# A bias table copied head by head within DRAM, and the last rows' final weighting taken apart, in a hybrid attention and mLSTM block

## The chip, the cores and the metric

The kernel runs on one core of a Trainium2 chip. The metric is the time of one execution on the device in microseconds (us). Engines are named as in the profile: PE (TensorE, matmuls), PEld (its weight loads), DVE (VectorE), ACT (ScalarE), POOL (GpSimd) and SP (SyncE, which here only issues DMAs).

## The reference, cut to what matters

One layer, 1024 rows of 1024 channels. The names that matter for the change are the relative-position bias, which is added to the scores of every head, and the last RMSNorm.

```
xn = rmsnorm(h, norm_w)
q, k, v, z, ml_q .. ml_z, ml_i, ml_f, gate_a, gate_m = split(xn @ w_in)
# differential attention, 8 heads, two score maps each
bias   = rel_bias[_rel_bucket(kpos - qpos)]            # 32 buckets x 8 heads
logits = q @ k.T + bias;  masked by chunks of 64
attn   = softmax(logits[0]) - lam * softmax(logits[1])
y_a    = rmsnorm(attn @ v, subln_w) * silu(z)
y_m    = mlstm(...) * silu(ml_z)
merged = sigmoid(gate_a) * (y_a @ w_pa) + sigmoid(gate_m) * (y_m @ w_pm)
h      = h + merged @ w_out
out    = rmsnorm(h, norm_final)
```

The bias depends on the distance between key and query alone, and is constant from a distance of 128 on. So one row of 384 numbers for each head holds it.

## The kernel before

Each projection is cut into *units* of 256 output columns: a unit's weights are loaded as two halves (`wt`, 3 buffers, L226), a power of two is found from their sum of squares (ACT L245 for the squares, DVE L159 for the sum `s`, one matmul with ones at L165, L135 to L139 for the scales `sb` and `isb`), and each half is split into a high and a low f16 part (`wp`, ACT L257 and DVE L259). Three matmuls replace one of f32 (`mm3`, L330 to L332; for units whose output stands in rows, L359 to L361). The units run in the order attention (for head h: `aqk` queries and keys, `avz` values and gate), attention gates, mLSTM, and so on; beside the units of head h+1 the attention of head h is computed, placed by a written list (PLAN_A). A scheduler then gives each engine a fixed order of instructions; engines wait for each other by semaphores. All DMAs of this part go out from SP, in SP's order: an issue that must wait holds those behind it.

`tables` (L408) makes the bias. A matmul gives `tb`, 8 heads on 8 partitions by 384 numbers (L428, L430, L431). One DMA (L433) writes it to DRAM as `tb_d`: each head's row of 1536 B 128 times, at a stride of 513 numbers. Read back at a stride of 512 (L590) this gives each of 128 query rows its own shift: the `strip` of a head, 128 x 256, two buffers. POOL scales it and puts the mask in (L591, L594), and the attention of that head begins with copying it into `BB` (DVE L806), from where L828 adds it to the scores. The projection of the input and forget gates (`if_proj`, L451; `wifp` is its weights' split) stands between the first two units.

The last stage (L1149 to L1179) multiplies by `w_out` in four blocks of 256 columns (`ch`), each over 8 row tiles (`tt`): L1170 adds the matmul's result to x in `xr`, L1171 sums its squares into `sso`. In the last block `factor` (L1131) makes the reciprocal root (a reduction on DVE, two small operations on POOL), and `finish` (L1138) weights the tile before: the left half on DVE, the right half on ACT and POOL, or on DVE too for the last tile; each half has its DMA (L1147).

Of the kernel before, what the change touches and what calls it, by code (L numbers as in the profile page):

```python
# [10 lines left out]
F32 = mybir.dt.float32  # L11
BF = mybir.dt.bfloat16
I32 = mybir.dt.int32
AF = mybir.ActivationFunctionType
ALU = mybir.AluOpType
AX = mybir.AxisListType

P = 128
S = 1024
D = 1024  # L20
NT = S // P
KC = D // P
H = 8
HD = 64
NB = 32
EPS = 1e-6
# [22 lines left out]
def block_kernel(ctx, tc, x, norm_w, w_in, lam, subln_w, rel_bias, conv_w, conv_b, b_if,  # L49
                 mh_w, b_gate, w_pa, w_pm, w_out, norm_final, onehot, out):  # L50
    nc = tc.nc
    v, s, g, te = nc.vector, nc.scalar, nc.gpsimd, nc.tensor
# [7 lines left out]
    dram = ctx.enter_context(tc.tile_pool(name="dram", bufs=1, space=bass.MemoryType.DRAM))  # L60
# [7 lines left out]
    def nm(p):  # L68
        uid[0] += 1
        return f"{p}{uid[0]}"  # L70

    def ctile(shape, dt=F32, p="c"):
        n = nm(p)
        return const.tile(shape, dt, tag=n, name=n)

    def R(dt=F32, shape=None, p="r"):
        return ring.tile(shape or [P, S], dt, tag="t4", name=nm(p))
# [7 lines left out]
    def sm(cols=1, dt=F32, p="s", bufs=6):  # L85
        return small.tile([P, cols], dt, tag=f"{p}{cols}", name=nm(p), bufs=bufs)

    def p_ps():
        return pp.tile([P, 512], F32, tag="pp", name=nm("pp"))
# [4 lines left out]
    def m_ps():  # L94
        return pmi.tile([P, 512], F32, tag="pmi", name=nm("pmi"))
# [4 lines left out]
    def junk(w):  # L100
        return wpool.tile([P, S], BF, tag="junk", name=nm("junk"), bufs=1)[:, :w]
# [171 lines left out]
    def wplain(w, i, c):  # L273
        hi, lo = w.parts[i // 2]
        return hi[:, i % 2, c], lo[:, i % 2, c]
# [127 lines left out]

    nlam = ctile([P, 1], p="nlam")
    lnc = ctile([P, 1], p="lnc")
    tb_d = dram.tile([H, P * 513], F32, tag="tbd", name="tb_d")

    def tables():  # L408
        oh = R(shape=[NB, 384], p="oh")
        nc.sync.dma_start(oh, onehot)  # L410
        lj = R(shape=[P, HD], p="lj")
        ls = sm(cols=2, p="ls")
        v.tensor_tensor_reduce(lj, lamb[:, 0, :], lamb[:, 1, :], 1.0, 0.0, op0=ALU.mult, op1=ALU.add,
                               accum_out=ls[:, 0:1])
        v.tensor_tensor_reduce(lj, lamb[:, 2, :], lamb[:, 3, :], 1.0, 0.0, op0=ALU.mult, op1=ALU.add,
                               accum_out=ls[:, 1:2])
        le = sm(cols=2, p="ls")
        s.activation(le, ls, AF.Exp)
        v.tensor_tensor(nlam, le[:, 1:2], le[:, 0:1], op=ALU.subtract)
        v.tensor_scalar(nlam, nlam, LAMBDA_INIT, None, op0=ALU.subtract)  # L420

        v.scalar_tensor_tensor(lnc, nlam, -1.0, nlam, op0=ALU.mult, op1=ALU.max)
        v.tensor_scalar(lnc, lnc, 1.0, 2.0 ** -5, op0=ALU.max, op1=ALU.mult)
        s.activation(lnc, lnc, AF.Ln)
        v.tensor_scalar(lnc, lnc, -1.0, None, op0=ALU.mult)
        yield
        tb_ps = m_ps()
        te.matmul(tb_ps[:H, :384], rb, oh, start=True, stop=True)  # L428
        tb = R(shape=[H, 384], p="tb")
        v.tensor_copy(tb, tb_ps[:H, :384])  # L430
        v.tensor_scalar(tb, tb, tb[:, 0:1], None, op0=ALU.subtract)  # L431

        nc.sync.dma_start(tb_d.rearrange("h (q u) -> h q u", u=513)[:, :, :384],  # L433
                    tb.unsqueeze(1).to_broadcast([H, P, 384]))
        yield
        cols_ps = m_ps()
        te.transpose(cols_ps[:, :NR], rows, ident[:NR, :NR])
        v.tensor_copy(cols, cols_ps[:, :NR])
        v.tensor_scalar(hb, cols[:, 88:104], 0.5, None, op0=ALU.mult)
        yield  # L440
# [116 lines left out]
    def sig_of(w):  # L557
        sg = sm(p="sig", bufs=8)
        v.tensor_tensor(sg, w.isb, isx, op=ALU.mult)
        return sg  # L560
# [18 lines left out]
    def c_aqk(h, w):  # L579
        sg = sig_of(w)  # L580
        v.tensor_scalar(sg, sg, 2.0 ** -60, None, op0=ALU.max)
        negc = sm(p="negc")
        v.scalar_tensor_tensor(negc, sg, -(2.0 ** 23), sg, op0=ALU.mult, op1=ALU.mult)
        sq = sm(p="sigm")
        v.tensor_tensor(sq, w.sb, sx, op=ALU.mult)
        v.tensor_scalar(sq, sq, 2.0 ** 60, None, op0=ALU.min)
        invc = sm(p="invc")
        v.scalar_tensor_tensor(invc, sq, 2.0 ** -23, sq, op0=ALU.mult, op1=ALU.mult)
        strip = ring.tile([P, 256], F32, tag="strip", name=nm("strip"), bufs=2)
        nc.sync.dma_start(strip, tb_d[h, :P * 512].rearrange("(q u) -> q u", u=512)[:, 127:383])  # L590
        g.tensor_scalar(strip, strip, invc, 1.0, op0=ALU.mult, op1=ALU.mult)  # L591
        mc = sm(p="mc")
        v.tensor_scalar(mc, invc, 2.0 ** 20, None, op0=ALU.min)
        g.tensor_scalar(strip[0:64, 192:256], maskv, mc[0:64, :], 1.0, op0=ALU.mult, op1=ALU.mult)  # L594
        Q = R(F16, [P, 2, S], p="Q")
        K = [R(F16, [P, 2, S], p="K") for _ in range(2)]
        live["qk", h] = (Q, K, negc, strip)
        hl = [None, None]
        done = [0, 0]

        def post(cb, th, ap):
            if hl[cb] is None:
                hl[cb] = R(F16, [P, 2, S], p="hl")
            t, x2 = HS[th], hl[cb]
            s.activation(x2[:, 0, t], ap, AF.Copy, scale=2.0 ** -13)
            v.scalar_tensor_tensor(x2[:, 1, t], ap, 2.0 ** -13, x2[:, 0, t], op0=ALU.mult,
                                   op1=ALU.subtract)
            done[cb] += 1
            if done[cb] == 2:
                for p in range(2):  # L610
                    src = x2[p * 64:p * 64 + 64]
                    for j in range(2):
                        if cb == 0:
                            nc.sync.dma_start(Q[j * 64:j * 64 + 64, p, :], src[:, j, :])
                        else:
                            nc.sync.dma_start(K[p][j * 64:j * 64 + 64, :, :], src)
        return None, post
# [162 lines left out]
    xr = []  # L780
# [278 lines left out]
    for _ in range(4):  # L1059
        first.prep_step()  # L1060
    weave(startup(0), first.prepping, normed(1))
    weave(startup(1), tables())


# [60 lines left out]
    nfb = BB  # L1125
    nc.sync.dma_start(nfb, norm_final.unsqueeze(0).to_broadcast([P, D]))
    sso = ctile([P, NT, 4], p="sso")
    last_bg.pop(0)()
    wo[0].finish_prep()

    def factor(tt):  # L1131
        rs = sm(p="xrs")
        v.tensor_reduce(rs, sso[:, tt, :], op=ALU.add, axis=AX.X)
        g.tensor_scalar(rs, rs, 1.0 / D, EPS, op0=ALU.mult, op1=ALU.add)
        g.tensor_tensor(rs, rs, mhalf[:, 0:1], op=ALU.pow)
        return rs

    def finish(tt, rs):  # L1138
        xt = xr[tt]
        for k in range(2):  # L1140
            c = HS[k]
            if k == 1 and tt < NT - 1:
                s.activation(xt[:, c], xt[:, c], AF.Copy, scale=rs)
                g.tensor_tensor(xt[:, c], xt[:, c], nfb[:, c], op=ALU.mult)
            else:
                v.scalar_tensor_tensor(xt[:, c], xt[:, c], rs, nfb[:, c], op0=ALU.mult, op1=ALU.mult)
            nc.sync.dma_start(out[0, tt * P:(tt + 1) * P, c], xt[:, c])  # L1147

    late = []  # L1149
    for ch in range(4):  # L1150
        w, so = wo[ch].w, [None, None]
        c = slice(ch * 256, ch * 256 + 256)
        n = 0
        for tt in range(NT):
            th, to = tt // 4, slice(tt % 4 * P, tt % 4 * P + P)
            ms = M[th][1]
            ps = p_ps()[:, :256]
            for _ in mm3(ps, KC, lambda i: (ms[i // 2][:, 0, i % 2, to], ms[i // 2][:, 1, i % 2, to]),
                         lambda i: wplain(w, i, slice(0, 256)), True, True):
                if last_bg:  # L1160
                    last_bg.pop(0)()
                n += 1
                if ch < 3 and n >= 2 and n % 3 == 0:
                    wo[ch + 1].start_prep()
                    wo[ch + 1].prep_step()
            if so[th] is None:
                so[th] = sm(p="so")
                v.tensor_tensor(so[th], w.isb, M[th][0], op=ALU.mult)
            xt = xr[tt]
            v.scalar_tensor_tensor(xt[:, c], ps, so[th], xt[:, c], op0=ALU.mult, op1=ALU.add)  # L1170
            s.activation(junk(256), xt[:, c], AF.Square, accum_out=sso[:, tt, ch:ch + 1])  # L1171
            if ch == 3:
                if len(late) > 0:
                    finish(*late.pop(0))
                late.append((tt, factor(tt)))
        if ch < 3:
            wo[ch + 1].finish_prep()
    for a in late:
        finish(*a)  # L1179

# [47 lines left out]
```

## Time and profile before

| | us |
|---|---|
| median of 3 runs (1415.33 to 1417.44) | 1416.35 |
| the profiled execution | 1417.01 |
| its span, first to last instruction | 1415.2 |
| PE busy | 1372.3 (97% of the span) |
| DVE busy | 848.1 (60%) |
| ACT busy | 734.3 (52%) |
| POOL busy | 157.1 (11%) |
| mean granted clock of PE | 0.993 of full speed |

The profile records one execution: for each engine when an instruction began and how long it took. An idle time is shown with the instruction that ended it. DMA share is the part of the time in which the core's 16 DMA engines were busy, on average. A busy PE is not the same as a fed PE, so the spacing of matmuls is read as well.

### The profile page before, as it was taken

To read this page: it belongs to the slowest core of one execution; us is meant where nothing else is said; L and a number is where in the kernel's file an instruction comes from. 1 tells how busy PE (TensorE), PEld (TensorE's weight loads), DVE (VectorE), ACT (ScalarE), POOL (GpSimd) and SP (SyncE) were. 2 spreads that over 40 slices of the span, in tenths; PEclk is the share of its full clock that TensorE was granted. 3 is DMA by queue.
4 is the path that set the end of the run, shared out by engine and by line. 5 is a ranking of instruction groups with operands and counts; after the bars stand their busy time and mean duration, and the time that the engine had idled before them with its cause. 6 is when DMAs were issued, how large, how long until landed. Compare 5 with 4: busy or idle time off the path is not lost.

```text
span 1415.2 us, 25057 instructions
## 1 busy us (share of the span) xinstructions
PE 1372.3 (97%) x9650; PEld 912.0 (64%) x9650; DVE 848.1 (60%) x2312; ACT 734.3 (52%) x1532; POOL 157.1 (11%) x215
## 2 busy tenths in 40 slices
PE   6979999999999999999999999999999999999997
PEld 3647576675765754444587696777768674444786
DVE  6267869769687677423627674765765654133633
ACT  7266657567675677622344443444435344544543
POOL 2001010010010001100102011020220200122004
PEclk9989999999999999999999999999999999999999
DMA  6557456474573534544221422322322135435203
GB/s 202 68 132 152 91 113 136 98 142 90 113 155 81 128 99 140 157 161 134 64 67 60 105 54 82 63 73 53 91 67 76 60 105 164 149 112 171 105 16 119
DMA packets 232761, 150.34 MB, mean 106 GB/s; under 512 B 117313, under 2 KB 209746, under 8 KB 232642
## 3 DMA queue, kind: packets, MB, share of 16 engines
q1 hardware_dynamic: 218482, 123.22, 35.5%
q10 hardware_dynamic: 14160, 25.53, 5.4%
q8 instruction: 75, 1.23, 0.4%
q14 instruction: 44, 0.36, 0.1%
HBM read 90.19 MB, written 18.68 MB: 77 GB/s over the span
## 4 chain that ended last, share of the span: by engine, by line
PE 78%; DVE 8%; DMA 5%; ACT 5%; issue 2%; POOL 2%; SPq 0%; POOLq 0%; DVEq 0%; ACTq 0%
PE pp L330 14%; PE pp L332 14%; PE pp L331 14%; PE pp L359 8%; PE pp L360 8%; PE pp L361 8%; PE psb L818 4%; DMA z<-z 2%; DMA wt<-in_w_in_dram 2%; DVE z L828 2%; ACT z L832 1%; DMA qw<-rows_d 1%; DVE z L851 1%; PE psb L914 1%; DVE wp L259 1%
## 5 line engine op out<-in xcount | busy, mean ns | idle before, releaser
L359 PE MATMUL pp<-wp,X 128*128 128x256 f16 x1280 | 350.2, 274 | 2.3 <-DVE tz L570 2.3
L361 PE MATMUL pp<-wp,X 128*128 128x256 f16 x1280 | 350.2, 274 | 0.0
L360 PE MATMUL pp<-wp,X 128*128 128x256 f16 x1280 | 350.2, 274 | 0.0
L332 PE MATMUL pp<-X,wp 128*128 128x512 f16 x768 | 291.0, 379 | 1.0 <-DVE wp L259 1.0
L330 PE MATMUL pp<-X,wp 128*128 128x512 f16 x768 | 291.5, 380 | 0.3 <-ACT wp L257 0.3
L331 PE MATMUL pp<-X,wp 128*128 128x512 f16 x768 | 291.5, 380 | 0.0
L257 ACT ACTIVATE wp<-wt,sb 128x512 f16<-128x512 f32 x208 | 137.5, 712 | 111.0 <-DVE sb L138 69.0
L245 ACT ACTIVATE junk<-wt 128x1024 bf16<-128x1024 f32 x112 | 118.2, 1056 | 115.6 <-DMA wt<-in_w_in_dram 105.2
L332 PEld LDWEIGHTS <-wp 128*128 128x128 f16 x1024 | 100.1, 98 | 119.1 <-DVE wp L259 1.5
L330 PEld LDWEIGHTS <-wp 128*128 128x128 f16 x1024 | 100.2, 98 | 101.8 <-issue 1.7
L331 PEld LDWEIGHTS <-wp 128*128 128x128 f16 x1024 | 100.1, 98 | 97.1
L259 DVE SCALAR_TENSOR_TENSOR wp<-wt,sb,wp 128x512 f16<-128x512 f32 x208 | 149.8, 760 | 13.4 <-ACT wp L257 11.8
L359 PEld LDWEIGHTS <-X 128*128 128x128 f16 x1280 | 125.7, 98 | 18.8 <-DVE tz L570 2.5
L360 PEld LDWEIGHTS <-X 128*128 128x128 f16 x1280 | 125.7, 98 | 16.0
L361 PEld LDWEIGHTS <-X 128*128 128x128 f16 x1280 | 125.7, 98 | 15.8
L832 ACT ACTIVATE z<-z,mx 128x256 f32<-128x256 f32 (+7 forms) x128 | 98.7, 772 | 46.9 <-DVE mx L831 27.4
L828 DVE CUSTOM_DVE_ANT_0 z<-psb,BB,negc 128x256 f32<-128x256 f32 (+7 forms) x128 | 104.1, 814 | 13.8 <-PE psb L818 13.7
L332 PE MATMUL pp<-Y,wp 128*128 128x512 f16 x256 | 97.0, 379 | 0.0
L331 PE MATMUL pp<-Y,wp 128*128 128x512 f16 x256 | 97.0, 379 | 0.0
L330 PE MATMUL pp<-Y,wp 128*128 128x512 f16 x256 | 97.0, 379 | 0.0
L655 DVE SCALAR_TENSOR_TENSOR acc<-up,wcol,acc 128x512 f32<-128x512 f32 x96 | 78.1, 828 | 27.1 <-POOL acc L656 24.8
L818 PE MATMUL psb<-K,Q 128*128 128x512 f16 (+3 forms) x384 | 83.3, 325 | 8.1 <-DVE mx L828 3.8
(253 smaller groups left out, 2005.0 us busy)
## 6 DMA issues: line engine op xcount, KB each, us to landing
wt<-in_w_in_dram SPq DMA_DIRECT2D x128, 256.0 KB, 3.3
wt<-in_w_in_dram SPq DMA_DIRECT2D x24, 512.0 KB
K<-hl SPq DMA_DIRECT2D x32, 256.0 KB, 4.2
gate_d<-tg ACTq DMA_DIRECT2D x32, 256.0 KB, 2.4
xt<-in_x_dram SPq DMA_DIRECT2D x8, 512.0 KB, 5.3
Q<-hl SPq DMA_DIRECT2D x32, 128.0 KB, 2.6
wt<-in_w_pa_dram SPq DMA_DIRECT2D x8, 512.0 KB, 3.8
ft<-gate_d ACTq DMA_DIRECT2D x16, 256.0 KB, 2.7
```

Of the source, the lines that this page charges most:

```text
L245: s.activation(j, w.wt[k], AF.Square, accum_out=ss[:, k:k + 1])
L257: s.activation(dst[0], src, AF.Copy, scale=w.sb)
L259: v.scalar_tensor_tensor(dst[1], src, w.sb, dst[0], op0=ALU.mult, op1=ALU.subtract)
L330: te.matmul(ps, wh, xh, start=(start and i == 0), stop=False, **kw)
L331: te.matmul(ps, wh, xl, start=False, stop=False, **kw)
L332: te.matmul(ps, wl, xh, start=False, stop=(stop and i == n - 1), **kw)
L359: te.matmul(ps[:, o], xh[:, t], wh, start=i == 0, stop=False)
L360: te.matmul(ps[:, o], xh[:, t], wl, start=False, stop=False)
L361: te.matmul(ps[:, o], xl[:, t], wh, start=False, stop=i == KC - 1)
L818: te.matmul(sp[:, c:e], Q[:, p, i * P:(i + 1) * P], K[p][:, j, c:e], start=(j == 0), stop=(j == 1))
L828: v.tensor_tensor_reduce(z[:, :n], sp[:, :n], bb[:, S - n:], negc, BIG, op0=ALU.add, op1=ALU.min, accum_out=mx)
L832: s.activation(z[:, :n], z[:, :n], AF.Exp, bias=mx, scale=-1.0, accum_out=rr[:, 2 * i + p:2 * i + p + 1])
```

## The change

**The table.** `tb` (8 rows of 384) goes to DRAM once, as `tbs_d`. A new function `table(h)` copies row h from there 128 times into a DRAM tensor of its own, `tb_d[h]`, with the stride of 513 as before. `table(0)` is called in `tables`, `table(h + 1)` behind the strip load of head h.

**The last rows.** For the last row tile the sum over the first three blocks, its scale and the product of columns 0 to 767 with `norm_final` are made before the last block (`early_part`). After the last block the remaining sum of squares is added within the scaling on POOL, without a reduction on DVE; then ACT multiplies columns 0 to 511 by the root, and DVE columns 768 to 1023 by root and weight, and 512 to 767 by the root.

```
-    tb_d = dram.tile([H, P * 513], F32, tag="tbd", name="tb_d")
+    tbs_d = dram.tile([H, 384], F32, tag="tbsd", name="tbs_d")
+    tb_d = {}
+    def table(h):
+        tb_d[h] = dram.tile([P, 513], F32, tag=f"tbd{h}", name=f"tb_d{h}")
+        nc.sync.dma_start(tb_d[h][:, :384], tbs_d[h:h + 1, :].to_broadcast([P, 384]))
...
-        nc.sync.dma_start(tb_d.rearrange("h (q u) -> h q u", u=513)[:, :, :384],
-                    tb.unsqueeze(1).to_broadcast([H, P, 384]))
+        nc.sync.dma_start(tbs_d, tb)
+        table(0)
...
-        nc.sync.dma_start(strip, tb_d[h, :P * 512].rearrange("(q u) -> q u", u=512)[:, 127:383])
+        nc.sync.dma_start(strip, tb_d[h].rearrange("q u -> (q u)")[:P * 512].rearrange("(q u) -> q u", u=512)[:, 127:383])
+        if h + 1 < H:
+            table(h + 1)
...
+    def early_part(tt):
+        rs = sm(p="xrs")
+        v.tensor_reduce(rs, sso[:, tt, :3], op=ALU.add, axis=AX.X)
+        g.tensor_scalar(rs, rs, 1.0 / D, EPS, op0=ALU.mult, op1=ALU.add)
+        for c in (slice(0, 384), slice(384, 768)):
+            g.tensor_tensor(xr[tt][:, c], xr[tt][:, c], nfb[:, c], op=ALU.mult)
+        return rs
...
     def factor(tt):
         rs = sm(p="xrs")
+        if tt == NT - 1:
+            g.tensor_scalar(rs, sso[:, tt, 3:4], 1.0 / D, last_rs, op0=ALU.mult, op1=ALU.add)
+        else:
...
     def finish(tt, rs):
         xt = xr[tt]
+        if tt == NT - 1:
+            s.activation(xt[:, :512], xt[:, :512], AF.Copy, scale=rs)
+            nc.sync.dma_start(out[0, tt * P:(tt + 1) * P, :512], xt[:, :512])
+            v.scalar_tensor_tensor(xt[:, 768:], xt[:, 768:], rs, nfb[:, 768:], op0=ALU.mult, op1=ALU.mult)
+            v.tensor_scalar(xt[:, 512:768], xt[:, 512:768], rs, None, op0=ALU.mult)
+            nc.sync.dma_start(out[0, tt * P:(tt + 1) * P, 512:], xt[:, 512:])
+            return
...
+        if ch == 2:
+            last_rs = early_part(NT - 1)
```

The scheduler's order differs in the first attention phase and at the end; in between it is the same. Three places matter. First SP, where the table is written. Before, the one write stands ahead of the second load of unit 2 (`wt_532`), and the first strip among the queries' DMAs:

```order
L226 DMA wt_458<-in_w_in_dram 128x4x128 [waits DMAHW4_49]
L433 DMA tb_d<-tb_356 1024x1x384 [waits DMAHW5_49,DVE_49]
L226 DMA wt_532<-in_w_in_dram 128x4x128 [waits DMAHW6_49,DVE_49]
L226 DMA wt_532<-in_w_in_dram 128x4x128 [waits DMAHW7_49]
L614 DMA Q_425<-hl_494 64x1024 [waits DMAHW0_49,Activation_49]
L590 DMA strip_419<-tb_d 128x256 [waits DMAHW5_49,DMAHW1_49]
L614 DMA Q_425<-hl_494 64x1024 [waits DMAHW2_49,DVE_49]
```

In the changed kernel (line numbers are the new file's: L438 writes `tbs_d`, L412 is `table`, L595 the strip load, `wt_536` that same load):

```order
L438 DMA tbs_d<-tb_356 8x384 [waits DMAHW5_49,DVE_49]
L412 DMA tb_d_360<-tbs_d 128x384 [waits DMAHW6_49,DMAHW5_49]
L412 DMA tb_d_423<-tbs_d 128x384 [waits DMAHW7_49]
L412 DMA tb_d_910<-tbs_d 128x384 [waits DMAHW0_49]
L412 DMA tb_d_1686<-tbs_d 128x384 [waits DMAHW1_49]
L595 DMA strip_421<-tb_d_360 128x256 [waits DMAHW6_49,DMAHW2_49]
L412 DMA tb_d_2462<-tbs_d 128x384 [waits DMAHW3_49]
L595 DMA strip_908<-tb_d_423 128x256 [waits DMAHW7_49,DMAHW4_49]
L412 DMA tb_d_3238<-tbs_d 128x384
L412 DMA tb_d_4014<-tbs_d 128x384
L412 DMA tb_d_4790<-tbs_d 128x384
L595 DMA strip_1684<-tb_d_910 128x256 [waits DMAHW0_49,DVE_49]
```

All eight copies and the first three strip loads have moved ahead of the load of `wt_536`, which is the next row. The third strip waits for DVE, since it takes the first strip's buffer.

The second place is DVE, where the strip of head 0 is copied into `BB`. Before, the copy (L806) follows the scales of unit 2:

```order
L159 TENSOR_TENSOR s_724<-wss_670 128x1 [waits Activation_49]
L135 TENSOR_SCALAR nb_728<-pmi_726 128x1 [waits PE_49]
L137 TENSOR_SCALAR nb_728<-nb_728 128x1 [waits DVE_49]
L138 TENSOR_SCALAR sb_722<-nb_728 128x1 [waits DVE_49]
L139 TENSOR_SCALAR isb_723<-nb_728 128x1
L806 COPY BB_95<-strip_419 128x256 [waits Pool_49]
L559 TENSOR_TENSOR sig_894<-isb_723,isx_120 128x1 [waits DVE_49]
```

In the changed kernel (L813) it stands among the scales of the gates' projection (`sb_436`) and of the unit `avz` of head 0 (`sb_482`), 25 rows earlier:

```order
L400 SCALAR_TENSOR_TENSOR X_396<-pmi_404,nws_134,X_396 128x512 [waits Activation_49]
L137 TENSOR_SCALAR nb_442<-nb_442 128x1 [waits DVE_49]
L135 TENSOR_SCALAR nb_488<-pmi_486 128x1 [waits PE_49]
L813 COPY BB_95<-strip_421 128x256 [waits Pool_49]
L138 TENSOR_SCALAR sb_436<-nb_442 128x1 [waits DVE_49]
L139 TENSOR_SCALAR isb_437<-nb_442 128x1
L137 TENSOR_SCALAR nb_488<-nb_488 128x1 [waits DVE_49]
L463 TENSOR_TENSOR sig_447<-isb_437,isx_120 128x1 [waits DVE_49]
L138 TENSOR_SCALAR sb_482<-nb_488 128x1 [waits DVE_49]
```

The copy waits for POOL, and so everything behind it on DVE, the splits `wifp` and `wp` of `avz` among them, waits for the strip.

The third place is the matmul with ones for unit 2's scales (L165) on PE. Before, it stands behind three of the four groups of unit `avz`:

```order
L361 MATMUL pp_782<-wp_523,X_394 128x256
L165 LDWEIGHTS ones_91 [waits DVE_49]
L165 MATMUL pmi_726<-s_724,ones_91 128x1 [waits PE_49]
L818 LDWEIGHTS Q_425 [waits DMAHW5_49,DMAHW6_49,DMAHW2_49,DMAHW0_49]
L818 MATMUL psb_921<-K_426,Q_425 128x128 [waits Activation_49]
L818 LDWEIGHTS Q_425
L818 MATMUL psb_921<-K_426,Q_425 128x128
L359 LDWEIGHTS X_325 [waits DVE_49]
```

In the changed kernel it stands in the second group, behind its first twelve matmuls, and the first two score matmuls (`psb`, here ahead of the fourth group) have moved into unit 2:

```order
L360 MATMUL pp_713<-wp_509,X_256 128x256
L361 LDWEIGHTS X_256
L361 MATMUL pp_713<-wp_509,X_256 128x256
L165 LDWEIGHTS ones_91 [waits DVE_49]
L165 MATMUL pmi_730<-s_728,ones_91 128x1 [waits PE_49]
L359 LDWEIGHTS X_288
L359 MATMUL pp_713<-wp_518,X_288 128x256
```

The matmul with ones, and with it the demand for the load, has moved ahead by 168 rows.

## Rows read from the trace of the kernel before

**Rows 1.** The page's slices: busy tenths of PE in 40 equal slices of 35.4 us
```profile
PE   6979999999999999999999999999999999999997
```

**Rows 2.** Timeline of PE: start us, us, line, operation, [idle before <-releaser]
```profile
50.48 1.91 PE L471 MATMUL psb<-X,wifp 128*32 128x512 f16 x32
52.32 0.28 PE L359 MATMUL pp<-wp,X 128*128 128x256 f16 x1
...
67.94 0.27 PE L361 MATMUL pp<-wp,X 128*128 128x256 f16 x1
...
72.22 0.18 PE L165 MATMUL pmi<-s,ones 128*128 128x1 bf16 x1 [4.00 <-DVE s L159]
76.19 0.37 PE L818 MATMUL psb<-K,Q 128*128 128x128 f16 x2 [3.79 <-ACT gif L473]
78.83 0.40 PE L359 MATMUL pp<-wp,X 128*128 128x256 f16 x1 [2.27 <-DVE tz L570]
...
86.94 0.38 PE L330 MATMUL pp<-X,wp 128*128 128x512 f16 x1
```

**Rows 3.** Timeline of SP's DMA queue, start us and us of the issue
```profile
34.20 0.81 SPq L433 DMA_DIRECT2D tb_d<-tb  x1
44.76 8.08 SPq L226 DMA_DIRECT2D wt<-in_w_in_dram  x2
...
68.85 0.36 SPq L590 DMA_DIRECT2D strip<-tb_d  x1
```

**Rows 4.** Chain of waits: start us, us, what
```profile
45.19 25.31 DMA wt<-in_w_in_dram
```

**Rows 5.** Windows: stretch us, length, busy us of each engine (x instructions), PEclk, DMA share, GB/s
```profile
38.00:40.00 2.00, 1.95 (x14) 1.27 (x13) 1.19 (x3) 1.12 (x3) 0.00 (x0) 1.00 0.46 49
...
74.00:76.00 2.00, 0.00 (x0) 0.10 (x1) 2.00 (x4) 2.00 (x4) 0.00 (x0) 0.50 1.03 242
...
90.00:100.00 10.00, 9.77 (x53) 4.61 (x51) 8.82 (x36) 7.20 (x20) 0.00 (x0) 1.00 0.21 42
...
688.00:689.00 1.00, 1.00 (x7) 0.45 (x5) 0.93 (x2) 1.00 (x2) 0.00 (x0) 1.00 1.13 286
```

**Rows 6.** Timeline of VectorE (DVE), 42 to 78 us
```profile
42.63 0.35 DVE L461 SCALAR_TENSOR_TENSOR wifp<-early,sb,wifp 128x128 f16<-128x128 f32 x1
...
43.31 2.74 DVE L259 SCALAR_TENSOR_TENSOR wp<-wt,sb,wp 128x512 f16<-128x512 f32 x4
...
72.95 0.28 DVE L806 COPY BB<-strip 128x256 f32<-128x256 f32 x1
...
76.89 0.34 DVE L828 CUSTOM_DVE_ANT_0 z<-psb,BB,negc 128x128 f32<-128x128 f32 x1
```

**Rows 7.** Timeline of POOL: the first strip
```profile
71.68 0.48 POOL L591 TENSOR_SCALAR strip<-strip,invc 128x256 f32<-128x256 f32 x1 [48.22 <-DMA strip<-tb_d]
72.26 0.31 POOL L594 TENSOR_SCALAR strip<-maskv,mc 64x64 f32<-64x64 f32 x1
```

**Rows 8.** The page's DMA issues: count, KB each, median us from issue to landing
```profile
wt<-in_w_in_dram SPq DMA_DIRECT2D x128, 256.0 KB, 3.3
...
gate_d<-tg ACTq DMA_DIRECT2D x32, 256.0 KB, 2.4
...
strip<-tb_d SPq DMA_DIRECT2D x8, 128.0 KB, 3.6
```

**Rows 9.** Timeline of the end, all engines
```profile
1388.92 0.19 POOL L1134 TENSOR_SCALAR xrs<-xrs 128x1 f32<-128x1 f32 x1 [87.10 <-DVE xrs L1133]
...
1407.88 0.72 ACT L1143 ACTIVATE xr<-xr,xrs 128x512 f32<-128x512 f32 x1 [1.32 <-POOL xrs L1135]
...
1408.68 1.27 POOL L1144 TENSOR_TENSOR xr<-xr,BB 128x512 f32<-128x512 f32 x1 [0.83 <-ACT xr L1143]
...
1410.04 0.19 POOL L1134 TENSOR_SCALAR xrs<-xrs 128x1 f32<-128x1 f32 x1
...
1410.89 1.42 DVE L1146 SCALAR_TENSOR_TENSOR xr<-xr,xrs,BB 128x512 f32<-128x512 f32 x2 [1.13 <-POOL xrs L1135]
```

More of the change, by code (lines that the diff above doesn't have):

```diff
@@ L1129, in block_kernel @@
     wo[0].finish_prep()
+    def early_part(tt):
[5 more added lines that the diff above has]
+        return rs
     def factor(tt):
         rs = sm(p="xrs")
-        v.tensor_reduce(rs, sso[:, tt, :], op=ALU.add, axis=AX.X)
-        g.tensor_scalar(rs, rs, 1.0 / D, EPS, op0=ALU.mult, op1=ALU.add)
+        if tt == NT - 1:
+            g.tensor_scalar(rs, sso[:, tt, 3:4], 1.0 / D, last_rs, op0=ALU.mult, op1=ALU.add)
+        else:
+            v.tensor_reduce(rs, sso[:, tt, :], op=ALU.add, axis=AX.X)
+            g.tensor_scalar(rs, rs, 1.0 / D, EPS, op0=ALU.mult, op1=ALU.add)
         g.tensor_tensor(rs, rs, mhalf[:, 0:1], op=ALU.pow)
@@ L1139, in finish @@
         xt = xr[tt]
+        if tt == NT - 1:
[5 more added lines that the diff above has]
+            return
         for k in range(2):
             c = HS[k]
-            if k == 1 and tt < NT - 1:
+            if k == 1:
                 s.activation(xt[:, c], xt[:, c], AF.Copy, scale=rs)
```

## The prediction

> **What bounds the kernel now.** I read the page's slices first: PE stands at 9 in almost every slice [rows 1], so a change pays where PE is not fed. Besides the first 35 us, only the third slice (70.8 to 106 us) falls to 7. The timeline of PE shows the hole [rows 2]: the matmuls run 0.109 us apart from 52.32 to 67.94 us ((67.94 - 52.32) / 143), then PE waits 4.00, 3.79 and 2.27 us, together 10.06. [...]
>
> What ends the hole: the first wait is for the sum of squares of unit 2's weights (s, L159). The chain of waits carries it through one weight load that took 25.31 us [rows 4]. Such a load usually lands 3.3 us after its issue [rows 8]. SP's timeline says why this one did not [rows 3]: the 1.5 MB write tb_d<-tb went out at 34.20, the load wt at 44.76 behind it (its two issues alone took 8.08 us), and the strip load, which waits for tb_d to land, could go at 68.85 only. So tb_d needed 34.6 us. In the window at 38 us it is alone: 49 GB/s, with the 16 DMA engines 0.46 busy [rows 5]. The load landed 1.7 us after tb_d (45.19 + 25.31 = 70.5).
>
> The second place is the end. There POOL sets the pace, and after the last reciprocal root VectorE weights both halves, 1.42 us [rows 9].
>
> **The change, part by part.** *The table.* The 1024 pieces of 1536 B that left eight partitions become one 12 KB store (tbs_d) and eight copies DRAM to DRAM of 128 such pieces. "Head by head" is not how they stand: SP has all eight copies and the first three strips ahead of unit 2's second load (wt_536). So this load still follows all the table's bytes, and the gain hangs on the copies' speed. Call R the time of one copy (0.197 MB). The trace of before has no such copy. Bounds: 0.7 us, if it runs like the window at 688 us, where row broadcasts from DRAM (L679, L681) and weight loads ran at 286 GB/s [rows 5]; 4.0 us, if the table's 49 GB/s is a limit of the writes as such, whoever makes them. Between them lies 2.0 us: each DMA engine keeps the old pace of a piece (0.46 of 16 busy, so some eight at work, 128 pieces each in 34.6 less 2.4 us, 0.25 us a piece) and sixteen share the work. I take 2.0: the same destination rows at the same odd stride of 2052 B are the nearest row.
>
> Why eight engines were at work the trace does not say. [...]
>
> [...] The window at 688 us, where six DMAs of 256 and 512 KB share 286 GB/s, does not look like transfers that wait for each other, but no copy from DRAM to DRAM is in this trace.
>
> With R = 2.0: tbs_d goes at 34.2 and lands 2.4 us later (as gate_d [rows 8]), 36.6. The first four copies are issued one behind the other, and their bytes are through at about 37.2 + 4 x 2.0 = 45.2. The first strip, issued when copy 0 has landed (about 40), queues behind copy 3 and lands near 47.6 (3.6 us alone [rows 8], less the part that overlaps). POOL scales it in 0.48 + 0.31 us [rows 7], and VectorE copies it into BB at about 48.8.
>
> *A new wait on VectorE.* That copy (0.28 us [rows 6]) stood at 72.95 us; now it stands ahead of the scales of the gate and value weights, so VectorE, free at about 42, waits 7 us for the strip. Behind it are wifp (42.63 before [rows 6], now about 50.2 when done) and the four wp splits (43.31 before, now from 50.4, 2.74 us). PE asks for wifp at 50.48 and for the first split at 52.32 [rows 2], for the second twelve matmuls later. All come in time: the wait is covered, just. ScalarE, which waits for the same scales, has nothing else that PE needs before 57.6.
>
> *The load itself.* wt_536 also waits for the third strip (its buffer is the first strip's, free after the copy at 48.8) and for the second split, 51.8. The copies' bytes end at 37.2 + 16 = 53.2, the strips add 1; the load lands at 54.2 + 3.3 = 57.5. Its squares take about 1.2 us, so s is there at 58.9. PE's matmul for it now stands 168 rows earlier, 12 matmuls into the second value group: 52.32 + 60 x 0.109 = 58.9. I put 0.3 us of waiting. With R = 0.7 nothing waits; the load lands near 51.
>
> *What follows.* PE then runs through its value groups to 52.32 + 192 x 0.109 = 73.3 and starts the next unit there instead of at 86.94: 13.6 us less 0.2 for two score matmuls that stood in the hole and now come after it, 13.4. No transfer is tied to an absolute time, so the rest moves along. A little is given back: VectorE did the first piece of attention in the hole (0.34 us [rows 6] and a small addition), now in a stretch where it is 0.88 busy beside a PE of 0.98 [rows 5]. I take 0.5 us, between 0 and 1.5.
>
> *The end.* The two early multiplications (2 x 384 / 512 x 1.27 = 1.9 us) and a scale of 0.19 fall on POOL, idle 87.10 us until 1388.92 [rows 9], within the 24 x 0.109 = 2.62 us in which PE makes the first tile of the last block: nothing. The dropped VectorE reduction gains nothing either: POOL comes from the tile before (1408.68 + 1.27) and started at 1410.04 for that reason [rows 9]. After the root ScalarE (0.72 us) and VectorE work side by side, 0.72 us instead of 1.42; but two DMAs now follow each other on SP, whose issue takes 0.36 for a like one [rows 3], so the last one goes 0.3 us earlier. Gain 0.3, between 0 and 0.7.
>
> Sum: -13.4 + 0.3 + 0.5 - 0.3 = -12.9. The profiled execution took 1417.0 (its span 1415.2), 0.65 above the median of 1416.35. 1417.0 - 12.9 = 1404.1, against the median 1403.5.
>
> **Rivals.**
> - *The copies are only half as good* (R = 2.4 to 3, 65 to 80 GB/s). [...] For it: the odd stride, and reading and writing DRAM at once. Against: twice the engines.
> - *The table still runs at 49 GB/s, and now it also holds VectorE* (R = 4.0). The first strip lands at about 55.6, VectorE copies at 56.8, wifp comes at 58.2: PE waits 7.7 us at 50.48. [...] For it: nothing in the trace shows writes to such rows faster. Against: 256 KB stores of gate_d land in 2.4 us [rows 8].
> - *The hole is refilled.* The load was late for another reason, or what PE needs after 73 us (scores from Q and K, whose DMAs stand behind the load on SP) comes no earlier than before: 1414 to 1416.5. Against: Q and K go once the outputs of unit 0 are split, about 60 us in the slow case, and K has 13 us to land.
>
> **How the numbers follow.** Forecast 0.74 (its own range 1401 to 1407), half as good 0.12, slower 0.07, refilled 0.07. What a measurement of this kernel can tell from no change is about 0.2%, 2.8 us. Faster: 0.74, most of 0.12, and 0.02 of the refilled: 0.87. Same: 0.06. Slower: 0.07. The range runs from 1400.5 (R = 0.7, nothing given back, the full 0.7 at the end, and the spread of runs) to 1411, the better half of the first rival: 0.80.
>
> **What would show it.** Right: PE's timeline shows no idle time over 1 us between 50 and 74 us, and the first L330 matmul of unit 2 near 73.5 instead of 86.94; clock 1.00 from 50 to 90; DMA share near 0.9 instead of 0.46 while the copies run; the copy into BB near 49 (near 44 with fast copies). Wrong: a wait of PE at the gate projection, or for s, of more than 3 us; the copies still ending after 60. At the end the last two output DMAs should be issued one right behind the other; a first scale of POOL that starts later after the last block's first tile would show that the early multiplications stand in the way.

## The result, and the profile after

The changed kernel took 1404.12 us (median of four runs, 1403.28 to 1405.13), the kernel before, on the same chip, 1416.17 (1415.33 to 1417.44): ratio 0.9914, 95% interval 0.9897 to 0.9932. Forecast were 1403.5 us, 1400.5 to 1411. The profiled execution has a span of 1402.9 us where before it was 1415.2: 12.3 less. In the page's slices the third one stands at 9, where it stood at 7 [rows 1]:

```profile
PE   6999999999999999999999999999999999999997
```

PE's timeline of the same stretch as in [rows 2] (start us, us, line, operation, idle before): no row has idle time in front until 91.79 us, and the first matmul of unit 2 starts at 73.13 instead of 86.94.

```profile
50.29 1.91 PE L476 MATMUL psb<-X,wifp 128*32 128x512 f16 x32
...
58.70 0.17 PE L165 MATMUL pmi<-s,ones 128*128 128x1 bf16 x1
...
73.13 0.38 PE L330 MATMUL pp<-X,wp 128*128 128x512 f16 x1
```

SP's queue shows the table (L412) and the load behind it (L226), which answer to [rows 3]: the load's two issues take 0.94 us where they took 8.08.

```profile
34.01 0.30 SPq L438 DMA_DIRECT2D tbs_d<-tb  x1
35.45 2.47 SPq L412 DMA_DIRECT2D tb_d<-tbs_d  x4
40.26 0.35 SPq L595 DMA_DIRECT2D strip<-tb_d  x1
40.65 0.47 SPq L412 DMA_DIRECT2D tb_d<-tbs_d  x1
41.22 0.53 SPq L595 DMA_DIRECT2D strip<-tb_d  x1
41.79 1.75 SPq L412 DMA_DIRECT2D tb_d<-tbs_d  x3
44.41 0.33 SPq L595 DMA_DIRECT2D strip<-tb_d  x1
47.06 0.94 SPq L226 DMA_DIRECT2D wt<-in_w_in_dram  x2
```

In the windows (columns as in [rows 5]; the last two are DMA share and GB/s) the copies run at 168 to 177 GB/s where the table ran at 49. At that pace one of 0.197 MB takes R = 1.1 to 1.2 us, not the 2.0 of the forecast. The third row holds the stretch of the old hole: PE is busy throughout, and its granted clock stays at 1.00, where it stood at 0.50 from 74 to 76 us [rows 5].

```profile
38.00:40.00 2.00, 1.95 (x13) 1.35 (x13) 1.19 (x3) 1.11 (x4) 0.00 (x0) 1.00 0.86 177
40.00:42.00 2.00, 1.95 (x12) 0.82 (x11) 1.83 (x6) 0.66 (x2) 0.00 (x0) 1.00 0.68 168
...
50.00:90.00 40.00, 39.93 (x319) 27.77 (x318) 22.36 (x77) 23.45 (x53) 0.79 (x2) 1.00 0.45 111
```

VectorE's wait for the first strip, ahead of the splits, is 2.27 us instead of the 7 forecast; the copy into BB that stood at 72.95 [rows 6] is at 44.09. The load's squares (ScalarE) begin at 51.93, s is there at 53.28 (53.12 + 0.16), and PE asks for it at 58.70.

```profile
44.09 0.29 DVE L813 COPY BB<-strip 128x256 f32<-128x256 f32 x1 [2.27 <-POOL strip L601]
...
44.94 0.35 DVE L466 SCALAR_TENSOR_TENSOR wifp<-early,sb,wifp 128x128 f16<-128x128 f32 x1
...
45.62 2.74 DVE L259 SCALAR_TENSOR_TENSOR wp<-wt,sb,wp 128x512 f16<-128x512 f32 x4
...
53.12 0.16 DVE L159 TENSOR_TENSOR s<-wss 128x1 bf16<-128x1 f32 x1 [4.04 <-ACT junk L245]
```

```profile
51.93 1.06 ACT L245 ACTIVATE junk<-wt 128x1024 bf16<-128x1024 f32 x1 [4.09 <-DMA wt<-in_w_in_dram]
```

At the end, the chain of the last row tile (all engines, against [rows 9]):

```profile
1376.64 0.19 POOL L1153 TENSOR_SCALAR xrs<-xrs 128x1 f32<-128x1 f32 x1 [1.54 <-DVE xrs L1152]
...
1393.38 1.26 POOL L1170 TENSOR_TENSOR xr<-xr,BB 128x512 f32<-128x512 f32 x1 [0.83 <-ACT xr L1169]
...
1396.38 1.27 POOL L1170 TENSOR_TENSOR xr<-xr,BB 128x512 f32<-128x512 f32 x1 [0.83 <-ACT xr L1169]
1397.64 0.27 POOL L1150 TENSOR_SCALAR xrs<-sso,xrs 128x1 f32<-128x1 f32 x1
...
1398.57 0.72 ACT L1160 ACTIVATE xr<-xr,xrs 128x512 f32<-128x512 f32 x1 [1.30 <-POOL xrs L1154]
1398.57 0.48 DVE L1162 SCALAR_TENSOR_TENSOR xr<-xr,xrs,BB 128x256 f32<-128x256 f32 x1 [1.84 <-POOL xrs L1154]
1398.97 0.35 DVE L1163 TENSOR_SCALAR xr<-xr,xrs 128x256 f32<-128x256 f32 x1
```

and SP's last issue:

```profile
1399.74 0.38 SPq L1164 DMA_DIRECT2D out_dram<-xr  x1
```

From POOL's first scale of the last block to the end of the span it is 1402.9 - 1376.64 = 26.26 us; before, 1415.2 - 1388.92 = 26.28 [rows 9]. The last rows' part gained nothing.

### The profile page after: what moved, and what is told of

Read it like the earlier page. It is cut to its first block, busy times and chain, and to the rows that moved or that the text cites. A ratio compares the mean times of both kernels' runs of the same rounds, so it can differ in the third digit from the quotient of the medians.

```text
span 1402.9 us, 25076 instructions
## 1 busy us (share of the span) xinstructions
PE 1371.0 (98%) x9650; PEld 911.3 (65%) x9650; DVE 846.4 (60%) x2312; ACT 735.5 (52%) x1533; POOL 158.9 (11%) x218
## 4 chain that ended last, share of the span: by engine, by line
PE 85%; DVE 6%; ACT 3%; DMA 2%; issue 2%; POOL 2%; SPq 0%; POOLq 0%; DVEq 0%; ACTq 0%
PE pp L330 15%; PE pp L331 15%; PE pp L332 15%; PE pp L359 9%; PE pp L361 9%; PE pp L360 9%; PE psb L825 4%; DVE z L835 2%; DMA z<-z 1%; PE psb L921 1%; DVE z L858 1%; PE pmi L940 1%; ACT z L839 1%; PE pmi L868 1%; PE psb L958 1%
## 5 line engine op out<-in xcount | busy, mean ns | idle before, releaser
L330 PE MATMUL pp<-X,wp 128*128 128x512 f16 x768 | 292.1, 380 | 0.3 <-ACT wp L257 0.3
L330 PEld LDWEIGHTS <-wp 128*128 128x128 f16 x1024 | 100.4, 98 | 102.2 <-issue 2.4
L259 DVE SCALAR_TENSOR_TENSOR wp<-wt,sb,wp 128x512 f16<-128x512 f32 x208 | 149.6, 759 | 13.4 <-ACT wp L257 11.8
L835 DVE CUSTOM_DVE_ANT_0 z<-psb,BB,negc 128x256 f32<-128x256 f32 (+7 forms) x128 | 104.1, 813 | 13.5 <-PE psb L825 13.5
L330 PE MATMUL pp<-Y,wp 128*128 128x512 f16 x256 | 97.0, 379 | 0.0
```

What stands on the lines that cost most here:

```text
L259: v.scalar_tensor_tensor(dst[1], src, w.sb, dst[0], op0=ALU.mult, op1=ALU.subtract)
L330: te.matmul(ps, wh, xh, start=(start and i == 0), stop=False, **kw)
L835: v.tensor_tensor_reduce(z[:, :n], sp[:, :n], bb[:, S - n:], negc, BIG, op0=ALU.add, op1=ALU.min, accum_out=mx)
```

## Experiments

Twelve runs of eleven kernels. Each ratio is to the kernel before on the same chip. The theory at the start: all of the gain is in the hole ahead of unit 2, because the table's bytes in front of unit 2's load now go fast; rivals on why they go fast, and on the tail, follow.

**The two parts of the change, each alone.** `table_only` has the last rows as before, `tail_only` the table as before.

```
table_only: without early_part, factor and finish as before
tail_only:  tb_d written in one DMA from tb as before
```

> This kernel has the table part of the change alone: the eight copies within DRAM, and the last rows' weighting as before. Main theory (the whole gain is in the hole ahead of unit 2): unit 2's first L330 starts at about 73.1 us as in the changed kernel, and the time is 1404 us, within 0.5 us of it; the tail's part of the change is worth 0 (its start was 12.28 us earlier than before and its end 12.3). Rival (the tail's part is worth the 0.3 us that was forecast, or up to 0.7): 1404.4 to 1404.8 us.

> This kernel has the last rows' part of the change alone: the table goes out in one transfer as before. Main theory: nothing is won, 1416.2 us within 0.3, unit 2's first L330 at about 86.9 us. Rival (tail worth 0.3 to 0.7): 1415.5 to 1415.9 us. If the early multiplications on POOL disturbed VectorE in the last passes, it would be over 1416.5.

Measured: table_only 1405.52 us (ratio 0.9921, interval 0.9908 to 0.9935), tail_only 1416.85 (1.0001, 0.9992 to 1.0010). From the last scale of a weight unit (L159) to the end of the span it is 47.8 us in table_only, 47.7 in tail_only, 47.8 before and after. table_only came out 1.5 us above its main theory and above both ranges, but its interval overlaps that of the changed kernel (0.9897 to 0.9932). So the table makes the whole difference, within 0.1% or so, and no gain of the tail's part is seen.

**One copy instead of eight, in two orders.** Both store the table once and copy it in one DMA within DRAM; the second differs in the outermost dimension alone.

```
one_copy:
+   nc.sync.dma_start(tb_d.rearrange("h (q u) -> q h u", u=513)[:, :, :384],
+                     tbs_d.unsqueeze(0).to_broadcast([P, H, 384]))
one_copy_heads_first:
+   nc.sync.dma_start(tb_d.rearrange("h (q u) -> h q u", u=513)[:, :, :384],
+                     tbs_d.unsqueeze(1).to_broadcast([H, P, 384]))
```

> The table is stored once (8x384), and one copy within DRAM writes all eight heads, with the 128 rows as the outermost dimension and the heads inside; the tail as in the changed kernel. Theory A (what was slow before was that the eight heads were the outermost dimension, so that about half of the DMA engines worked): the copy's 1.57 MB go at 120 to 170 GB/s with a DMA share of 0.8 or more, it is through by 47 to 50 us, unit 2's first L330 stands at 73 us, and the time is 1404 to 1405 us. Rival B (it is the splitting head by head that helps, since only small copies stand ahead of the first strip and of the weight load): 1408 us or more. Rival C (one large transfer still holds the weight load, but through the hole's slack): the load lands under 58 us and PE does not wait, though VectorE waits 5 us or more for the strip.

> As the kernel with one copy, but with the eight heads as the outermost dimension of the one copy within DRAM. Theory A (the outermost dimension of eight sets how many engines work): DMA share about 0.46 and about 49 GB/s while it runs, as in the kernel before; the weight load lands late, unit 2's first L330 at 85 to 88 us, and the time is 1415 to 1418 us. Rival B (the kernel before was slow because its source lay in eight partitions of SBUF, and a source in DRAM is fast): share 0.8 or more, over 120 GB/s, 1404 to 1405 us.

Measured: one_copy 1404.51 us (0.9917, 0.9903 to 0.9930). Neither splitting by head nor copying early for the first strip is needed: the strip goes at 47.28 us, after the whole copy, and VectorE's wait of 4.25 us falls behind its splits. Window of 38 to 44 us:

```profile
38.00:44.00 6.00, 5.91 (x33) 2.95 (x31) 5.12 (x21) 3.79 (x8) 0.00 (x0) 1.00 0.99 211
```

With the heads outermost it took 1411.56 us (0.9962, 0.9946 to 0.9977), which neither theory had. The same window:

```profile
38.00:44.00 6.00, 5.91 (x35) 3.20 (x34) 4.53 (x18) 3.80 (x7) 0.00 (x0) 1.00 0.56 160
```

The share, 0.56, is that of about half the 16 engines, where one_copy has 0.99. But the rate is 160 GB/s and not 49, so theory A falls: the number of engines was not what held the table. The load was in time too: s at 53.28 us. The 7 us that are lost against one_copy stand on PE, whose timeline still has two of the three waits of [rows 2]:

```profile
69.08 0.17 PE L165 MATMUL pmi<-s,ones 128*128 128x1 bf16 x1
...
73.06 0.37 PE L819 MATMUL psb<-K,Q 128*128 128x128 f16 x2 [3.82 <-ACT gif L474]
...
75.71 0.40 PE L359 MATMUL pp<-wp,X 128*128 128x256 f16 x1 [2.27 <-DVE tz L571]
...
82.93 0.38 PE L330 MATMUL pp<-X,wp 128*128 128x512 f16 x1
```

Unit 2 starts at 82.93 us where one_copy has it at 73.45. Here the scheduler left PE's order as before: L165, the matmul with ones for s, is PE's row 621, behind three value groups; in the changed kernel and in one_copy it is row 453. The scales of unit 2's weights come from it, and what follows them (ScalarE's gates, VectorE's four splits) takes longer than the one value group that is left to cover it. This is read from the two timelines; no run moves that one row alone.

**The load made late again, with the new order.** Sixteen or 24 more copies of the same kind, into rows that nobody reads, ahead of copy 0.

```
+        for k in range(16):        # or 24
+            extra = dram.tile([P, 513], F32, tag=f"tbx{k}", name=f"tb_x{k}")
+            nc.sync.dma_start(extra[:, :384], tbs_d[k % H:k % H + 1, :].to_broadcast([P, 384]))
         table(0)
```

> The changed kernel with 16 more copies of the same kind ahead of copy 0, into rows that nobody reads (3.1 MB). On SP, unit 2's second load stands behind 18 copies, the first strip behind the load; on PE and VectorE the order around the hole is that of the changed kernel (the matmul with ones for s in the second value group), but VectorE copies the strip into BB only ahead of s. Theory (the gain hangs on when the load and the strip land, with a slack of about 5.8 us: s is there at 53.1, PE asks at 58.9, and each us beyond that is a us of PE): with 1.1 us a copy the bytes are through at about 57, the load lands near 60, s is there at 61 to 63, PE waits 2 to 4 us, and the time is 1406 to 1409 us. Rival (copies of one queue don't add up, since they were not the limit): s before 58, no wait, 1404 us. By the forecast's 2.0 us a copy, the bytes would be through at 73, PE would wait 17 us, and the time would be 1420 or more.

> As the kernel with 16 more copies, but with 24 (4.7 MB). Theory: bytes through at about 65 to 66, s at 69 to 71, which is 1 to 3 us before the time at which the kernel before had it; PE waits 10 to 12 us for it in one piece and the clock falls: 1415 to 1420 us, so about the time of before. That would show that the late table alone makes up the whole difference. Rival (the other order of PE's work is what pays, also with a late load): 1410 us or less.

Measured: extra16 1413.44 us (0.9978, 0.9969 to 0.9987), extra24 1416.71 (1.0003, 0.9994 to 1.0013). The copies run at 172 GB/s (extra16, 44 to 52 us), 1.1 us each. PE's waits in extra16:

```profile
63.62 0.18 PE L165 MATMUL pmi<-s,ones 128*128 128x1 bf16 x1 [4.12 <-DVE s L159]
...
83.53 0.27 PE L828 MATMUL psb<-K,Q 128*128 128x128 f16 x2 [2.23 <-DVE mx L838]
```

and in extra24:

```profile
70.75 0.19 PE L165 MATMUL pmi<-s,ones 128*128 128x1 bf16 x1 [11.64 <-DVE s L159]
```

The waits for s are as expected (2 to 4, and 10 to 12 us), and extra24 came out at the time of before. extra16 came out 4.4 us above the upper end of what I said. The wait does not come alone: the granted clock falls to 0.59 in 64 to 68 us,

```profile
64.00:68.00 4.00, 4.00 (x25) 2.89 (x23) 3.01 (x16) 3.66 (x6) 0.00 (x0) 0.59 0.87 213
```

so that from L165 to unit 2's first L330 it takes 16.1 us instead of 14.4, and a second wait of 2.23 us follows in the attention. A table so late that PE waits 4.1 us for s cost some 9 in all. How much of the second wait comes from the late strip and VectorE's other order was not separated.

**Why the old table was slow.** Three kernels that write the table from SBUF: each head by itself from its one partition (`sbuf_heads`), and the one DMA of before with the eight rows on every fourth or every second partition.

```
sbuf_heads:
-   nc.sync.dma_start(tb_d[h][:, :384], tbs_d[h:h + 1, :].to_broadcast([P, 384]))
+   nc.sync.dma_start(tb_d[h][:, :384].rearrange("(o q) u -> o q u", o=1),
+                     tb_s[0][h:h + 1, :].unsqueeze(1).to_broadcast([1, P, 384]))
every_fourth (every_second: 2 and f=2):
+   v.tensor_copy(rb4.rearrange("n (h f) -> n h f", f=4)[:, :, 0], rb)
+   te.matmul(tb_ps[:4 * H, :384], rb4, oh, start=True, stop=True)
...
+   tb.rearrange("(h f) u -> h f u", f=4)[:, 0:1, :].to_broadcast([H, P, 384])
```

> Each head's copy is written straight from its one partition of SBUF (128 pieces of 1536 B), without the store to DRAM; copies 0 and 1 stand ahead of the first strip and of the load. PE's order around the hole is that of before (the matmul with ones behind three value groups), so that even with fast copies it would be at the 1411.6 us of the kernel with the heads outermost and a source in DRAM. Theory A' (what was slow before is reading one row of SBUF over and over: 49 GB/s from eight partitions, 6.1 GB/s from each): copy 0 takes about 32 us, the first strip lands at about 70, and the time is 1414 to 1430 us. Rival (the SBUF source is no limit): copy 0 takes 1 to 2 us and the time is about 1411.6 us.

> The table as in the kernel before, in one transfer from SBUF with the heads outermost, but its eight rows lie on partitions 0, 4, 8, ... 28 instead of 0 to 7 (the matmul that makes them has 32 columns, 24 of them zero); the last rows as in the changed kernel. PE's order around the hole is that of before. Theory P (what limited the table was the path out of SBUF that neighbouring partitions share: partitions 0 and 1 alone gave 27 GB/s with a DMA share of 0.86, partitions 0 to 7 gave 49): now the table runs at 150 to 200 GB/s, as the copy from DRAM with the same eight outermost did (160), s is there at about 53 us, and the time is 1411.6 us within 1. [...] Rival Q (each single row read over and over has its own limit, 49 / 8 = 6.1 GB/s): still 49 GB/s, 1416.6 us.

> The same with the rows on partitions 0, 2, 4, ... 14. Theory P: twice the rate of before, 90 to 110 GB/s; the table is through at 52 to 54 us, the load behind it lands by 56, s at 57 to 58, ahead of PE's demand at 69: 1411.6 us within 1.5, like the row on every fourth partition. Rival Q: 49 GB/s and 1416.6 us.

The window of 38 to 44 us, in sbuf_heads (copies 0 and 1, from partitions 0 and 1), then every_second, then every_fourth:

```profile
38.00:44.00 6.00, 5.90 (x35) 3.30 (x34) 4.29 (x16) 3.65 (x7) 0.00 (x0) 1.00 0.86 27
```

```profile
38.00:44.00 6.00, 5.91 (x33) 2.95 (x31) 5.12 (x21) 3.80 (x8) 0.00 (x0) 1.00 0.49 97
```

```profile
38.00:44.00 6.00, 5.90 (x33) 2.97 (x32) 5.12 (x21) 3.79 (x8) 0.00 (x0) 1.00 0.53 179
```

27, 49 (before, partitions 0 to 7 [rows 5]), 97 and 179 GB/s. Between the last three only the partitions differ: the same bytes, the same destination, about half of the engines at work each time (shares of 0.46, 0.49 and 0.53). Rival Q (each row has a limit of its own) falls, since the same eight rows go at three rates; what limited the table depends on how close together its rows lie. Spread twice as far they go 2.0 times as fast (97 to 49 GB/s), four times as far 3.7 times (179 to 49). That agrees with theory P; the path itself no run shows. The 179 GB/s are near what the copies from DRAM reach, 160 to 211; no run tells what limits there.

The times: sbuf_heads 1476.10 us (1.0419, 1.0401 to 1.0436). My 32 us for copy 0 were wrong (the strip that waits for it goes at 44.98 us, 9.5 after the first issue; two copies shared 27 GB/s where I had counted 6.1 for each), and so was 1414 to 1430: the loss comes later, where head by head the slow copies stand among the transposing DMAs of `z` on SP. PE's waits for those make 21.7 us in all, 2.5 before; that is 19 of the 59 us by which the span is longer, and the rest was not traced. every_fourth took 1413.59 us (0.9980, 0.9970 to 0.9989), every_second 1414.01 (0.9985, 0.9974 to 0.9995): s at 52.40 and 55.50 us, and in both the waits of 3.8 and 2.3 us that belong to PE's order of before. The times are 2.0 and 2.4 us above the 1411.6 expected from one_copy_heads_first, so both expectations of the time were missed; the profiled executions of the three (spans 1410.8, 1411.3, 1410.4) differ by less.

**The early part for all row tiles.** In the last block each row tile takes 3.0 us (POOL's L1170 to L1170, 1393.38 to 1396.38) where PE needs 2.62: root, ScalarE's scaling, POOL's product and the next root form a ring. `all_early` uses the change's early sum and early product for all eight tiles.

```
+            if ch == 2:
+                early_rs[tt] = early_part(tt)
...
+        s.activation(xt[:, :768], xt[:, :768], AF.Copy, scale=rs)
+        v.scalar_tensor_tensor(xt[:, 768:], xt[:, 768:], rs, nfb[:, 768:], op0=ALU.mult, op1=ALU.mult)
```

> The changed kernel, with its treatment of the last rows used for all eight row tiles: partial sum and product of columns 0 to 767 with the weight before the last block, after the root only ScalarE's scaling of 0 to 767 and VectorE's weighting of 768 to 1023. Main theory (in the last block each tile takes 3.02 us, since POOL multiplies 512 columns by the weight, 1.27 us, within the ring root, scaling, product, next root; PE needs 2.62): POOL's ring falls to about 2.5 us, PE's 2.62 sets the pace, and the kernel ends 7 x 0.4 = 2.8 us earlier, at 1401.3 us (1400.5 to 1402.5). Rival (the sixteen early products on POOL, 16 us, disturb VectorE or come too late): 1404 us or more. Rival (VectorE's own ring of weighting, residual, square and root keeps about 2.8 us): 1402.5 to 1403.5.

> The same kernel once more, beside the changed kernel on one chip, since four runs left 1401.7 to 1404.8 us. Main theory: from the last scale to the end of the span it takes 45.7 us, where the changed kernel takes 47.75, so it is 2 us faster than the changed kernel in the median: about 1402 to 1402.5. Rival (the scatter of single executions swallows it): the same median within 0.5 us.

> The changed kernel itself, unchanged, for comparison on the same chip: 1404.1 us within 0.7. In its first profile TensorE's clock fell to 0.66 of full speed at 521 us after a wait of 2.0 us, which cost 1.7 us; if that belongs to single executions and not to the kernel, a second profile may lack it, with a span near 1401.2 us.

Measured: all_early took 1403.27 us (ratio 0.9907, 0.9892 to 0.9922) and again 1402.07 (0.9904, 0.9891 to 0.9918), beside which the changed kernel took 1405.16 (0.9920, 0.9907 to 0.9934). Expected were 1401.3 (1400.5 to 1402.5) for the first and 1404.1 within 0.7 for the changed kernel: both missed. The first lies in the range of the rival with VectorE's ring of 2.8 us, but the pace of 2.62 us in the rows below speaks against that ring. Over all runs the medians are 1402.1 (eight) and 1404.8 (nine). POOL's timeline in all_early: it now waits for ScalarE's square, and a tile takes PE's 2.62 us.

```profile
1391.19 0.27 POOL L1149 TENSOR_SCALAR xrs<-sso,ers 128x1 f32<-128x1 f32 x1 [1.72 <-ACT junk L1189]
1391.54 0.55 POOL L1150 TENSOR_TENSOR xrs<-xrs,mhalf 128x1 f32<-128x1 f32 x1
1393.81 0.27 POOL L1149 TENSOR_SCALAR xrs<-sso,ers 128x1 f32<-128x1 f32 x1 [1.72 <-ACT junk L1189]
```

From the last unit's scale (L159) to the end of the span it takes 45.7 us in both profiles instead of 47.7: 2.0 of the 2.8 us expected. The intervals of the two kernels overlap; the 2.0 us are shown in the profiles, the exact gain over the changed kernel is not. The clock has a part in it: five of the eight executions of all_early have a mean granted clock of 0.998 or more, but only three of the changed kernel's nine, and among these the median spans are 1400.2 and 1401.5 us, 1.3 apart.

## Why the prediction was right, and which terms were off

- **The copies' speed (R).** 2.0 us were taken, 1.1 measured. The term that was off is "each DMA engine keeps the old pace of a piece (0.25 us)": that pace was not the engines' own, since with about half of them at work the table left SBUF at 49, 97 or 179 GB/s, by how far apart its rows lay. That sixteen engines would share the copies was an assumption that no row of before shows; the DMA share was 0.86 and 0.68 in the changed kernel's two windows, and 0.99 in one_copy's. Splitting the table lost no time here: eight copies and one, both through within PE's slack, gave the same time (1404.1 and 1404.5 us).
- **VectorE's wait and the load.** 7 us became 2.27, and s came at 53.3, not 58.9, ahead of PE's demand (58.70; forecast 58.9). Both follow from R, and both were covered, as said, so that the error in R moved the time by 0.3 us at most. In part this is luck: at R = 2.0 the forecast had no slack left, and any R below it gives nearly the same time, so the hit says little for the 2.0.
- **What follows.** Forecast: unit 2 at 73.3 us instead of 86.94, 13.4 gained. Measured 73.13, with L476 0.19 us earlier than its counterpart L471 in [rows 2]: 13.6. But the text put the whole hole down to the late load, and that is only a part of the reason. With the load in time and PE's order of before, 3.82 and 2.27 us of waiting stay (1411.6 us, 5.0 gained of 12); with the new order and a late load (s at 70.5) nothing is gained (1416.7). The whole gain needs both, the load in time and the new order, in which the matmul with ones stands 168 rows earlier. The sum came out right because it was made on the new order.
- **Given back.** Forecast 0.5 (0 to 1.5). The shift of the unit scales (L159) against before is 13.5 us at 111 us, 13.2 at 505, 11.4 at 537, and 12.3 at the end. The 1.8 between 505 and 537 are not VectorE's work, as I had put it, but go with a fall of the clock, which the section on the hardware shows. In the profiles of one_copy and all_early, where it did not fall there, unit 2 starts 13.5 and 13.6 us earlier than before, and the last unit scale stands 13.0 and 13.3 earlier: 0.5 and 0.3 given back, near the forecast.
- **The tail.** Forecast 0.3, measured 0.0 (26.28 and 26.26 us). The early products were free, as said; after the root the last DMA is issued earlier in the chain (its issue ends 23.48 us after POOL's first scale, before 23.74), but lands no earlier. Why the landing didn't follow was not tried. The page's last slice stands at 7 before, too [rows 1], which the prediction's first paragraph passes over, and it still does.
- **Rivals.** "Still at 49 GB/s" and "half as good" fell on the windows. "The hole is refilled" fell as well, but PE's order of before would have refilled more than half of it (7 of 12 us). The upper end of the range, 1411, rests on "half as good", and no run shows what that rival comes to. What a late load costs extra16 shows: with 4.1 us of waiting for s the loss was about 9, 1.7 of it on the slow clock behind the wait (0.59) and 2.2 in a second wait.

In the sum: forecast -13.4 + 0.3 + 0.5 - 0.3 = -12.9; measured -13.6 + 0 + 1.3 - 0 = -12.3 in the profiled executions, where the 1.3 hold the fall of the clock, which the forecast did not have.

## What to carry to other kernels

When a transfer holds up loads behind it, look at both its share and its rate: half the engines busy (0.46) at 49 GB/s and half the engines busy (0.53) at 179 GB/s are different faults. The table here, eight rows read out of SBUF 128 times each, went at 49 GB/s from neighbouring partitions and at 179 from every fourth; stored to DRAM once and copied there, at 168 to 177. For a table like it, rows further apart or the way through DRAM are worth a try. And a wait that is taken away gives only what the instruction order lets it give: look in the order for how much work stands between the instruction that waits and the next one that needs its result.

## What was not expected of the hardware

The rate of the table's DMA from SBUF followed the spread of its source's partitions (27 GB/s from partitions 0 and 1, 49 from 0 to 7, 97 from every second, 179 from every fourth), while in the two copies from DRAM the share of the engines went from 0.56 to 0.99 and the rate only from 160 to 211 GB/s, in the same window of 38 to 44 us.

A wait of 2 us on PE, about 522 us in, was followed by a fall of the granted clock in some profiles and not in others. It lasts 1.98 to 1.99 us in the six profiles in which the hole is closed: the changed kernel, its second run (to 0.80 in 521 to 525 us and 0.78 in 525 to 529) and table_only, where the clock fell, and one_copy and both of all_early, where it did not (the second of these has 1.00 from 504 to 528 us). In seven of the others, before among them, the wait at this place is 1.86 us, and the clock stayed at 1.00; sbuf_heads has no such wait there. The wait in the changed kernel, in the first profile of all_early and in the kernel before:

```profile
521.29 1.02 PE L825 MATMUL psb<-K,Q 128*128 128x512 f16 x4 [1.98 <-DVE mx L835]
```

```profile
522.06 1.02 PE L825 MATMUL psb<-K,Q 128*128 128x512 f16 x4 [1.99 <-DVE mx L835]
```

```profile
534.37 1.02 PE L818 MATMUL psb<-K,Q 128*128 128x512 f16 x4 [1.86 <-DVE mx L828]
```

Window of the changed kernel, and its two unit scales around it:

```profile
521.00:525.00 4.00, 3.71 (x12) 1.42 (x12) 2.89 (x7) 2.89 (x5) 0.00 (x0) 0.66 1.12 292
```

```profile
505.41 0.16 DVE L159 TENSOR_TENSOR s<-wss 128x1 bf16<-128x1 f32 x1 [1.27 <-ACT junk L245]
...
537.38 0.16 DVE L159 TENSOR_TENSOR s<-wss 128x1 bf16<-128x1 f32 x1 [1.36 <-ACT junk L245]
```

It cost 1.7 us: between these two scales it takes 32.0 us in the three profiles with the fall, and 30.2 to 30.3 in the ten others that have the wait. With three falls in six profiles of the closed hole and none in seven of the open one, the 1.7 us may be a price of the change that it pays in some executions; what decides on the fall stays open.
